# Three banks for scores, the norm factor and the inverse sums through DRAM, and gates ahead of the last branch's products, in a two-layer hybrid encoder

## The chip, the cores and the metric

The kernel runs on one core of a Trainium2 chip. The metric is device time in microseconds (us), lower is better. The time before is 1617.49 us, the median of three runs from 1617.4 to 1617.58. A core has TensorE for matrix products, VectorE (DVE), ScalarE (ACT) and GpSimd (POOL) for elementwise work, and SyncE (SP), which here only issues DMAs. TensorE writes its results into PSUM, which has eight banks of 128x512 float32; other data lie in SBUF.

## The reference

Two layers act on x, which has 512 tokens and 1024 channels, in float32. Per layer:

```python
h = rms_norm(x, attn_norm_g)
c_q, c_kv, k_rope, gq, gk, gv, pool_in, gate_logits = split_columns(h @ w_in, IN_SIZES)
o_mla = mla_branch(...)    # latent attention, 8 heads, keys of 64 + 32 rotary, values of 64
o_gqa = gqa_branch(...)    # grouped attention, 8 heads on 2 key heads of 64, axial rotary
o_pool = pool_branch(...)  # centred means over 2/4/8/16 tokens less the token, a 128x128 map per group
gates = sigmoid(gate_logits).reshape(b, s, 3, d)
merged = (gates[:, :, 0] * (o_mla @ w_branch_mla) + gates[:, :, 1] * (o_gqa @ w_branch_gqa)
          + gates[:, :, 2] * (o_pool @ w_branch_pool))
x = x + merged @ w_out
hf = rms_norm(x, ffn_norm_g)
u = depthwise_conv(hf @ ffn_w_up, ffn_conv_w, ffn_conv_b)      # width 3
x = x + (silu(u[..., :D_FF]) * u[..., D_FF:]) @ ffn_w_down     # D_FF = 2816
```

The attentions are softmax(q k^T / sqrt(d)) v, with a per-head RMS norm on queries and keys. `rms_norm` divides by the root mean square over the channels: one factor per token.

## The kernel before

**Precision.** Each operand of a large product is held as a sum of a high and a low part, and `mm3` issues three matmuls (high x high, high x low, low x high). Weights come from DRAM in pieces of up to 128x512, two to a load as a rule; `w_dma` issues the loads on SP into three rotating buffers (`RAW`), and `w_split` makes the high part on ACT (line 214) and the low part on DVE or POOL (line 221), three pieces ahead of use (`LA`). A load waits until the buffer it takes has been split, and SP runs its DMAs strictly in the order they were written.

**Order.** The program is one long Python function that puts out instructions in an order of its own. A `Clock` keeps planned times for each engine; `chain` puts out the steps of an evacuation one after another as the planned times come, and `ps(tag)` hands out PSUM banks by planned times. The banks have tags: `acc` two, `ST` two, `AV` two, `S` one, `mi` one. The chip takes nothing from the plan but the order on each engine; real waits go by semaphores.

**Stages of a layer.** The latent projection; four pool channel groups; the query, key and value projections; the attentions; the output projection (`w_out`); the up-projection of 44 blocks, which uses `acc`, `ST` and `AV` in turn (six banks); the down-projection. A block of 128 output channels takes 24 matmuls of 128x512 (8 input chunks, three each), on 512 tokens.

**The norm factor.** `norm_finish` sums squares with four small matmuls, takes the mean on DVE and the power -1/2 on POOL (`rt`, one factor per token, with tokens on partitions). Products with channels on partitions need it as a row repeated on all partitions: `rbc`. Before, DVE builds diagonal matrices of the factor's two parts (`dgh`, `dgl`) and `norm_rows` multiplies them with a matrix of ones on TensorE, two matmuls, and copies the result on ACT. There are four such norms. First users: the pool groups' evacuation (`pool_steps`) and `up_evac`.

**The attentions.** `attention` lists, per head, its steps at positions from `PLAN`: `t_q`, `t_k` (operands), `s_max` (scores by query in bank `S`; DVE takes their maxima `nm`, which go as a row through a DMA on ACT's queue), `probs` (four score tiles by key; ACT takes exp, ACT or DVE the high part `ph`, DVE the low part `pl`, and DVE the value sum `vt` of a column that has no room in the value matrix), `av_hi`, `av_lo`, `av_rest` (products with the values in a bank `AV`; the last, with `vt`, closes the head) and `o_out`. In `o_out`, after each second head, DVE transposes the sums of the pair in blocks, takes inverses and transposes them back; POOL multiplies the pair with them (DVE for the last pair) and the pair is split for the branch product.

**Filler.** Between these steps a `Filler` puts units of other work on TensorE: gate blocks (`gate`, 8 units of three matmuls), branch products (`branch`, 4 units), and the latent attention's query, key and value units (`make_q`, `make_n`, `make_v`). Where a step's inputs would not be ready by plan, up to `SLACK` more units are taken. `_order(br)` lists a branch's gates and products; `LAG` is how many gates go ahead of the first product (2: pool branch, 1: grouped, 0: latent, the last). The last figure of each `PLAN` row is the position at which the filler is to be used up. A `make_` unit is woven in at every second unit of the other work.

## Time and profile before

The profiled execution took 1617.62 us, of which the profile's span covers 1615.8. DMA engines moved 161.23 MB, 100 GB/s on average.

| engine | busy us | share of the span | instructions |
|---|---|---|---|
| TensorE matmuls (PE) | 1604.7 | 99% | 7155 |
| TensorE weight loads (PEld) | 1315.5 | 81% | 7155 |
| DVE | 949.8 | 59% | 1548 |
| ACT | 779.0 | 48% | 1407 |
| POOL | 1002.1 | 62% | 889 |

How to read the rows: line numbers are those of the kernel. A row of a group names line, engine, operation, tile written <- tiles read, shapes and count; then the busy time and the mean of one in ns, or min/median/max in ns with the first and last start in us. A row of waits reads "engine, instruction <- whom it waited for: total us, times, longest us". A row of a window reads "from:to length, busy time (instructions), granted clock of TensorE as a share of full speed, busy share of the DMA engines, GB/s"; with more engines, the busy times stand in the order PE, PEld, DVE, ACT, POOL. A row of a timeline reads start, duration, engine, line, operation, tiles, count, and in brackets the idle time before it and what ended it. DMA rows give KB and the median time from issue to landing in us.

### The profile page before, as it was taken

Reading aid. Unit: us, or ns where it says so; the run is one execution under the profiler, and the core shown is the slowest. Engines: PE = TensorE matmul, PEld = TensorE weight load, DVE = VectorE, ACT = ScalarE, POOL = GpSimd, SP = SyncE. Lnnn points to the kernel's source line nnn. Section 1 sums busy time; section 2 is a strip of 40 time slices with the busy share of each in tenths; the row PEclk is TensorE's granted clock in tenths of the full one; section 3 lists DMA queues with packets and bytes.
Section 4 is the critical chain, followed back from the end, with each engine's and each line's share of the span. In section 5 each row is a group of like instructions: output and inputs, shape, how many; then the busy total and the mean of one; then the engine's idle time right before and its main releaser. Section 6 shows DMA issues by size and latency. Waiting matters only on the chain.

```text
span 1615.8 us, 20557 instructions
## 1 busy us (share of the span) xinstructions
PE 1604.7 (99%) x7155; PEld 1315.5 (81%) x7155; DVE 949.8 (59%) x1548; ACT 779.0 (48%) x1407; POOL 1002.1 (62%) x889
## 2 busy tenths in 40 slices
PE   9999999999999999999999999999999999999999
PEld 8888878877888888888888887788778888888888
DVE  6768867865276666611047678777652766666000
ACT  6357766663444444423244576666633444444221
POOL 3764986854666665654477559668547566666542
PEclk9999999999999999999999999999999999999999
DMA  5232234414323223333333322343142222223331
GB/s 194 94 100 71 76 112 127 111 56 143 103 90 93 92 92 102 95 115 101 104 105 94 96 76 75 95 125 118 56 153 92 90 93 92 92 92 104 117 112 46
DMA packets 72104, 161.23 MB, mean 100 GB/s; under 512 B 12224, under 2 KB 33216, under 8 KB 72000
## 3 DMA queue, kind: packets, MB, share of 16 engines
q1 hardware_dynamic: 67104, 159.71, 31.5%
q8 instruction: 56, 0.92, 0.2%
q10 hardware_dynamic: 4896, 0.21, 0.2%
q14 instruction: 48, 0.39, 0.1%
HBM read 147.76 MB, written 12.06 MB: 99 GB/s over the span
## 4 chain that ended last, share of the span: by engine, by line
PE 95%; DVE 2%; POOL 1%; ACT 1%; issue 0%; DMA 0%; ACTq 0%; POOLq 0%; DVEq 0%
PE ps_acc L353 43%; PE ps_ST L353 24%; PE ps_AV L353 23%; PE ps_S L353 4%; PE ps_mi L353 2%; DVE pl L221 0%; DVE vt L225 0%; POOL MQ L221 0%; POOL wl L221 0%; ACT ps_ST L214 0%; ACT ph L214 0%; DVE gt L221 0%; DMA prm<-prm 0%; POOL osum L249 0%; POOL qa L221 0%
## 5 line engine op out<-in xcount | busy, mean ns | idle before, releaser
L221 POOL TENSOR_TENSOR wl<-raw,wh 128x512 fp32r<-128x512 f32 (+2 forms) x502 | 659.1, 1323 | 467.2 <-ACT wh L214 374.5
L214 ACT ACTIVATE wh<-raw 128x512 fp32r<-128x512 f32 (+1 forms) x521 | 309.4, 607 | 131.2 <-PE ps_ST L353 41.0
L225 DVE SCALAR_TENSOR_TENSOR a<-u,prm,a 128x512 f32<-128x512 f32 x176 | 238.8, 1358 | 79.4 <-ACT a L214 75.1
L353 PE MATMUL ps_acc<-HH,wh 128*128 128x512 f32 x592 | 234.2, 396 | 1.3 <-ACT mns L214 1.2
L353 PE MATMUL ps_acc<-HL,wh 128*128 128x512 f32 x592 | 234.5, 396 | 0.0
L353 PE MATMUL ps_acc<-HH,wl 128*128 128x512 f32 x592 | 233.9, 395 | 0.0
L353 PEld LDWEIGHTS ps_acc<-HH,wh 128*128 128x128 f32 x592 | 111.4, 188 | 27.6 <-ACT mns L214 1.4
L353 PEld LDWEIGHTS ps_acc<-HH,wl 128*128 128x128 f32 x592 | 111.2, 188 | 26.6
L353 PEld LDWEIGHTS ps_acc<-HL,wh 128*128 128x128 f32 x592 | 111.3, 188 | 25.7
L353 PE MATMUL ps_AV<-HL,wh 128*128 128x512 f32 x288 | 114.1, 396 | 0.0
L353 PE MATMUL ps_AV<-HH,wl 128*128 128x512 f32 x288 | 114.1, 396 | 0.0
L353 PE MATMUL ps_AV<-HH,wh 128*128 128x512 f32 x288 | 113.4, 394 | 0.0
L214 ACT ACTIVATE ps_ST<-ps_ST 128x512 f32<-128x512 f32 x128 | 74.2, 581 | 81.1 <-PE ps_ST L353 78.1
L221 POOL TENSOR_TENSOR al<-a,ah 128x512 fp32r<-128x512 f32 x44 | 58.1, 1320 | 84.9 <-ACT ah L214 56.5
L229 DVE TENSOR_REDUCE nm<-ps_S 128x1 fp32r<-128x512 f32 x128 | 87.5, 684 | 38.3 <-PE ps_S L353 37.3
L221 DVE TENSOR_TENSOR pl<-ps_ST,ph 128x512 fp32r<-128x512 f32 x128 | 86.6, 681 | 35.1 <-ACT ph L214 34.2
L353 PE MATMUL ps_ST<-HL,wh 128*128 128x512 f32 x240 | 95.2, 397 | 0.0
L353 PE MATMUL ps_ST<-HH,wl 128*128 128x512 f32 x240 | 94.9, 395 | 0.0
L353 PE MATMUL ps_ST<-HH,wh 128*128 128x512 f32 x240 | 94.5, 394 | 0.0
L214 ACT ACTIVATE a<-u,prm 128x512 f32<-128x512 f32 x88 | 71.8, 815 | 33.4 <-DVE u L221 33.4
L214 ACT ACTIVATE ah<-a 128x512 fp32r<-128x512 f32 x44 | 27.8, 632 | 116.0 <-DVE u L249 110.6
L214 ACT ACTIVATE a<-a 128x512 f32<-128x512 f32 x44 | 27.8, 632 | 112.9 <-DVE u L249 112.9
(372 smaller groups left out, 3654.9 us busy)
## 6 DMA issues: line engine op xcount, KB each, us to landing
raw<-w SPq DMA_DIRECT2D x228, 512.0 KB, 3.5
raw<-w SPq DMA_DIRECT2D x13, 384.0 KB, 3.1
XM<-x SPq DMA_DIRECT2D x16, 256.0 KB, 4.0
dtq<-tr SPq DMA_DIRECT2D x16, 192.0 KB, 3.2
dtk<-tr SPq DMA_DIRECT2D x16, 192.0 KB, 4.0
tf<-dtq SPq DMA_DIRECT2D x48, 64.0 KB, 2.8
tf<-dtk SPq DMA_DIRECT2D x48, 64.0 KB, 2.7
raw<-w SPq DMA_DIRECT2D x6, 448.0 KB, 3.4
```

What stands on the lines that cost most here:

```text
L214: return self.eng.activation(out, in_, func, **k)
L221: return self.eng.tensor_tensor(out, *a)
L225: return self.eng.scalar_tensor_tensor(out, *a)
L229: return self.eng.tensor_reduce(out, in_, *a, **k)
L353: PE.matmul(o, lhsT=lhsT, rhs=rhs, start=start, stop=stop)
```

## The change

- *Banks.* `probs` takes its bank from the tag `ST` or `mi`, whichever the plan frees sooner (`soonest`), so three banks serve score tiles. The first step of the value sum (key tile 0) is done by ACT in place of DVE.
- *Norm factor.* `dgh`, `dgl`, `norm_rows` and its matmuls are gone. SP writes `rt` as a row of 512 to DRAM (`row`) and reads it back repeated on 128 partitions into `rbc` (`rows`).
- *Inverse sums.* For the pairs that end with heads 1, 3 and 5, SP writes the two rows of sums to DRAM, reads them as 128x8 (`few`), DVE takes the reciprocal, SP writes it back and reads each row repeated on 64 partitions into `turned`; POOL multiplies with that. The pair of head 7 stays as it was.
- *Filler.* `LAG[0]` is 8 in place of 6: all eight gates of the last branch precede its products. The latent plan's filler ends at 35.5 in place of 33.91. Key and value units are woven in at every fourth unit (`gap`), query units at every second as before.

```diff
@@ -32,7 +32,7 @@
 EXTRA = (("q", 2, (2, 5)), ("n", 2, (6, 7)), ("v", 1, (2, 5)))
 
 SOONER = {1: 3 * KC, 0: 6 * KC}
-LAG = {2: 1, 1: 4, 0: 6}
+LAG = {2: 1, 1: 4, 0: 8}
 PRO = 0.47
 PRE_A = 16
 PRE_B = 8
@@ -41,7 +41,7 @@
 RSQRT_BITS = 1597463007.0
 SLACK = 35
 PLAN = {"gqa": (-4.2, -1.0, -0.2, 0.0, 0.65, 2.411, 4.57, 32.003),
-        "mla": (-6.2, -2.9, -1.0, 0.1, 0.64, 1.678, 1.82, 33.91)}
+        "mla": (-6.2, -2.9, -1.0, 0.1, 0.64, 1.678, 1.82, 35.5)}
 
 D_ROW, D_OUT, D_IN = 3.4, 3.2, 4.0
 REST = 0.4
@@ -228,8 +228,8 @@
         self._two(in_)
         return self.eng.tensor_reduce(out, in_, *a, **k)
 
-    def tensor_scalar(self, out, *a, psum=False):
-        self._count(out, *((0.0043, 0.2) if self.kind == "Pool" else (0.00105 if psum else 0.00055, 0.07)))
+    def tensor_scalar(self, out, *a):
+        self._count(out, *((0.0043, 0.2) if self.kind == "Pool" else (0.00055, 0.07)))
         return self.eng.tensor_scalar(out, *a)
 
     def tensor_copy(self, out, in_, psum=False):
@@ -288,6 +288,13 @@
         uid[0] += 1
         t = pp.tile([P, T], F32, tag=tag, name=f"ps_{tag}_{uid[0]}", bufs=nbank[tag])
         return t
+
+    def soonest(*tags):
+
+        for t in tags:
+            while not banks[t]:
+                ck.pop()
+        return min(tags, key=lambda t: banks[t][0])
 
     def free(tag):
         heapq.heappush(banks[tag], ck.fin + ck.SEM)
@@ -453,30 +460,23 @@
         for b in range(4):
             mm(s2[:, 2 * b:2 * b + 2], sq[:, b * P:b * P + P], f(ones[:, :2]), True, True)
         rt = out["rt"] = small("rt", [P, 8])
-        rh, rl = small("rth", [P, 8], F32R), small("rtl", [P, 8], F32R)
-        dg = out["dg"] = slot("dgh", F32R), slot("dgl", F32R)
+        rbc = out["rbc"] = slot("rbc")
+        d = dp.tile([T], F32, tag=f"rt{gen}", name=f"rt{gen}")
 
         def mean():
             V.tensor_scalar(rt, s2[:, :8], 1.0 / D, EPS, ALU.mult, ALU.add)
             free("S")
 
-        def diag(n):
-            r = f((rh, rl)[n]).rearrange("p (b t) -> p b t", t=2)[:, :, 0:1]
-            V.tensor_tensor(dg[n][:, :T].rearrange("p (b q) -> p b q", b=4), bc(ident[:, None, :], [P, 4, P]),
-                            bc(r, [P, 4, P]), ALU.mult)
-
-        chain(mean, *rsqrt_steps(rt, 8, ("rt", gen)), lambda: V.tensor_copy(rh, rt),
-              lambda: V.tensor_tensor(rl, rt, f(rh), ALU.subtract), lambda: diag(0), lambda: diag(1),
-              lambda: done("dg", gen), after=0.4)
-
-    def norm_rows(gen, out, tag):
-
-        need(("dg", gen))
-        r = ps(tag)
-        for n in range(2):
-            mm(r, ones, out["dg"][n][:, :T], n == 0, n == 1)
-        rbc = out["rbc"] = slot("rbc")
-        chain(lambda: (A.activation(rbc[:, :T], r, AF.Copy), free(tag), done("rbc", gen)))
+        def row():
+            SY.dma_start(d.rearrange("(b p) -> p b", p=P), rt.rearrange("p (b t) -> p b t", t=2)[:, :, 0])
+            ck.fin = ck.now + D_ROW
+
+        def rows():
+            SY.dma_start(rbc[:, :T], d.partition_broadcast(P))
+            ck.fin = ck.now + D_IN
+            done("rbc", gen)
+
+        chain(mean, *rsqrt_steps(rt, 8, ("rt", gen)), row, rows, after=0.4)
 
     def copy(out, in_, psum=True, bias=C_BIAS):
 
@@ -677,8 +677,6 @@
                 if l == 0 and g == 0 and n == 5:
                     norm_finish(G1, sq, nrm)
                     latents()
-            if g == (l == 0):
-                norm_rows(G1, nrm, "acc")
             chain(*pool_steps(g, acc, ptags[g]))
 
 
@@ -884,15 +882,15 @@
                     merged[m] = (mh, ml)
                     chain(product, add, *split(mh[:, :T], ml[:, :T], XM[:, m, :]), fin)
 
-            extra, tick = None, 0
+            extra, tick, gap = None, 0, 2
             for k, m in _order(br):
                 if k in mla_make:
-                    extra, tick = mla_make[k](m), 0
+                    extra, tick, gap = mla_make[k](m), 0, 2 if k == "q" else 4
                     continue
                 work = branch(m) if k == "b" else gate(m)
                 more = True
                 while more:
-                    if extra and tick % 2 == 0:
+                    if extra and tick % gap == 0:
                         if next(extra, END) is END:
                             extra = None
                         yield
@@ -1206,7 +1204,8 @@
                 need(key("m", h), key("q", h))
                 if not gqa:
                     need(key("kl", h))
-                sc = ps("ST")
+                tag = soonest("ST", "mi")
+                sc = ps(tag)
                 kb_ = slice(k * P, k * P + P)
                 if gqa:
                     mm(sc, s["ka"][:, kb_], s["qa"][:, :T], True, False)
@@ -1233,12 +1232,12 @@
 
                     if k == 0:
                         s["t"] = slot("vt", F32R)
-                        V.tensor_scalar(s["t"][:, :T], sc, vals(h, k)[1], None, ALU.mult, psum=True)
+                        A.activation(s["t"][:, :T], sc, AF.Copy, scale=vals(h, k)[1])
                     else:
                         t = s["t"][:, :T]
                         V.scalar_tensor_tensor(t, sc, vals(h, k)[1], f(t),
                                                ALU.mult, ALU.add)
-                    free("ST")
+                    free(tag)
                     if k == 3:
                         done(*key("t", h))
 
@@ -1301,14 +1300,34 @@
                     odst[h // 2] = (oh, ol)
 
                     turned, inv = slot("otr"), small("oinv", [P, 16])
+                if h in (1, 3, 5):
+                    few = small("few", [P, 8])
+                    d1, d2 = (dp.tile([2, T], F32, tag=f"s{n}{kind}{l}{h}", name=f"s{n}{kind}{l}{h}") for n in (1, 2))
+
+                    def line(out, in_):
+                        SY.dma_start(out, in_)
+                        ck.fin = ck.now + D_ROW
+
+                    def both():
+                        for j in range(2):
+                            SY.dma_start(turned[64 * j:64 * j + 64, :T], d2[j].partition_broadcast(64))
+                        ck.fin = ck.now + D_IN
+
+                    steps += [lambda: line(d1, sums[0:65:64, :T]),
+                              lambda: line(few, d1.rearrange("h (a e) -> (h a) e", e=8)),
+                              lambda: V.reciprocal(few, few),
+                              lambda: line(d2.rearrange("h (a e) -> (h a) e", e=8), few), both, add,
+                              lambda: G.tensor_tensor(raw[:, :T], raw[:, :T], turned[:, :T], ALU.mult),
+                              *split(oh[:, :T], ol[:, :T], raw[:, :T], eng=G), lambda: done(okey, l, h // 2)]
+                elif h == 7:
                     steps += [lambda: V.transpose(turned[:, :T], sums[:, :T]),
                               lambda: V.reciprocal(inv, turned[:, :T].rearrange("p (b f) -> p b f", f=32)[:, :, 0])]
                     steps += [add, lambda: (A.activation(inv[32:64], inv[0:32], AF.Copy),
                                             A.activation(inv[96:128], inv[64:96], AF.Copy))]
                     steps += [lambda: V.transpose(sums[:, :T].rearrange("p (b f) -> p b f", f=32),
                                                   bc(inv.unsqueeze(2), [P, 16, 32]))]
-                    steps += [lambda: (V if h == 7 else G).tensor_tensor(raw[:, :T], raw[:, :T], sums[:, :T], ALU.mult),
-                              *split(oh[:, :T], ol[:, :T], raw[:, :T], eng=V if h == 7 else G),
+                    steps += [lambda: V.tensor_tensor(raw[:, :T], raw[:, :T], sums[:, :T], ALU.mult),
+                              *split(oh[:, :T], ol[:, :T], raw[:, :T], eng=V),
                               lambda: done(okey, l, h // 2)]
                 chain(*steps)
 
@@ -1341,14 +1360,15 @@
                 if fn is s_max:
                     return [key("q", h)] + [key("kh", h)] * (not gqa), "S"
                 if fn is probs:
-                    return [key("m", h), key("q", h)] + [key("kl", h)] * (not gqa), "ST"
+                    return [key("m", h), key("q", h)] + [key("kl", h)] * (not gqa), ("ST", "mi")
                 if fn is av_hi:
                     return [key("ph", h, k)], "AV" if k == 0 else None
                 return [key("t", h)] if fn is av_rest else [key("pl", h, k)], None
 
             def waiting(fn, *args):
                 keys, tag = waits(fn, *args)
-                return not ck.has(*keys) or (tag and not (banks[tag] and banks[tag][0] <= ck.now))
+                tags = (tag,) if isinstance(tag, str) else tag or ()
+                return not ck.has(*keys) or bool(tags) and not any(banks[t] and banks[t][0] <= ck.now for t in tags)
 
             f0, first = fill.done, plan[0][0]
             for pos, fn, args in plan:
@@ -1466,8 +1486,6 @@
                 run(feat_major(acc, G2))
                 if n == 1:
                     norm_finish(G2, sq, fin)
-                if n == 2:
-                    norm_rows(G2, fin, "mi")
                 up_evac(c, part, acc, tag)
 
         last = l == L - 1
```

## The prediction

> **What bounds the kernel now.** I read the page first (the busy table, the chain that ended last), then TensorE's own waits, then windows cut around each wait, then the DMA and queue tables.
>
> ```profile
> span 1615.8 us, 20557 instructions
> ...
> PE 1604.7 (99%) x7155; PEld 1315.5 (81%) x7155; DVE 949.8 (59%) x1548; ACT 779.0 (48%) x1407; POOL 1002.1 (62%) x889
> ...
> PE 95%; DVE 2%; POOL 1%; ACT 1%; issue 0%; DMA 0%; ACTq 0%; POOLq 0%; DVEq 0%
> ```
>
> TensorE is the bound: 95% of the chain runs on it. So only two things can shorten the run: fewer matmuls, or fewer stalls between them. The 99% hides part of the stalls, because a matmul counts as busy until its modelled end, so I count starts instead. In each window below the matmuls in brackets include those still draining at its left edge (one; two in 973.68, where they are narrow); the others started in it.
>
> ```profile
> 505.79:517.00 11.21, 11.21 (x49) 1.00 0.29 91
> 240.11:241.17 1.06, 0.40 (x2) 1.00 0.97 397
> 356.23:358.25 2.02, 1.23 (x4) 1.00 0.05 18
> 365.69:367.27 1.58, 1.23 (x4) 1.00 0.00 0
> 973.68:975.47 1.79, 0.61 (x4) 1.00 0.87 119
> 1003.66:1005.11 1.45, 0.97 (x4) 1.00 0.00 0
> 1021.08:1027.26 6.18, 5.25 (x18) 1.00 0.25 86
> 1045.12:1046.16 1.04, 0.40 (x2) 1.00 0.10 24
> 1161.22:1163.25 2.03, 1.24 (x4) 1.00 0.00 0
> 1170.68:1172.27 1.59, 1.24 (x4) 1.00 0.85 268
> ```
>
> The first row is steady work: 48 starts in 11.21 us, 0.2335 us each, at full granted clock (1.00). The stall in another window is its length less 0.2335 per start.
> - 240 and 1045: one start each, 0.83 and 0.81 us lost. This is a latent value unit before its second half.
> - 356 and 1161: three starts, 1.32 and 1.33. The last head of the latent attention.
> - 365 and 1170: three starts, 0.88 and 0.89. The first product of the last branch.
> - 973: two starts, 1.32 (one is half as wide, so a little more). A latent key unit in layer 1.
> - 1003 and 1021: three and 17 starts, 0.75 and 2.21. The end of layer 1's grouped attention.
>
> That is 10.34 us in nine places. Whom TensorE waits for there:
>
> ```profile
> PE ps_AV L353 <- DVE vt L225: 1.7, 3, 0.8
> PE ps_acc L353 <- DVE vm L221: 1.3, 2, 0.7
> PE ps_acc L353 <- ACT mns L214: 1.2, 1, 1.2
> PE ps_ST L353 <- DVE vt L225: 0.5, 1, 0.5
> PE ps_acc L353 <- DVE ol L221: 0.5, 2, 0.2
> ```
>
> All are evacuations of a PSUM bank, or products of one, by DVE or ACT; none is a weight or a DMA.
>
> **The change part by part.**
>
> *Norm factor through DRAM.* Four norms each lose two matmuls of 128x512 that spread the factor over the partitions.
>
> ```profile
> L353 PE MATMUL ps_acc<-dgh,ones x2: 392/392/393, 35.1 to 830.0; 128*128 128x512 f32 x2
> L353 PE MATMUL ps_mi<-dgh,ones x2: 396/398/399, 449.1 to 1254.2; 128*128 128x512 f32 x2
> L221 POOL TENSOR_TENSOR rt<-rt,mhalf x4: 1644/1652/1655, 28.4 to 1248.9; 128x8 f32<-128x8 f32 x4
> L214 ACT ACTIVATE rbc<-ps_acc x2: 577/578/580, 36.4 to 830.9; 128x512 f32<-128x512 f32 x2
> L214 ACT ACTIVATE rbc<-ps_mi x2: 598/599/600, 449.8 to 1254.9; 128x512 f32<-128x512 f32 x2
> ```
>
> They are on the path, in the stream of starts: 8 x 0.2335 = 1.87 us gained. The Trainium skill (TensorE: Matmul & The Clock Gate, "Back-to-back issue gap") gives 512/2.4 + 2.5 = 216 ns for such a step; by it the gain would be 1.73, and the measured step decides. On DVE four casts, four subtractions and eight 128x512 products go, on ACT four copies; neither was waited for. Instead SP issues a write of 512 elements and a broadcast read of 256 KB. Nearest rows:
>
> ```profile
> qb<-nm ACTq DMA_DIRECT2D x16, 2.0 KB, 2.1
> gb<-gb SPq DMA_DIRECT2D x2, 256.0 KB, 4.8
> tf<-dtp SPq DMA_DIRECT2D x24, 64.0 KB, 2.9
> DMA to landing us min/median/max: 1.9/1.9/4.2
> ```
>
> (The last row is that of the tile nm.) In the feed-forward the power ends near 445.5 and the factor came at 450.4. Now the write also waits on SP behind one weight load, up to a block (24 x 0.2335 = 5.6 us), then 1.9 to 4.2 and 2.9 to 4.8: factor at 450.3 to 460.1. The first bank that needs it back is the seventh in turn, six blocks (33.6 us) after 437, so at about 470: cost 0, cover 10 us even at the late end. ACT and DVE are queued behind the late factor and the weight splits stand behind them on ACT; three pieces are split ahead (8.4 us), and the code's own plan already allows 3.4 + 4.0 us for the two hops, so I take 0. At the start of a layer it is tighter, since the latent transposes wait for DVE work queued behind the factor's first use:
>
> ```profile
> 41.42 3.99 DVE L233 TENSOR_SCALAR mx<-mx,ssc 128x256 f32<-128x256 f32 x8 [0.93 <-POOL ssc L221]
> 46.75 1.03 PE L357 MATMUL ps_acc<-C,mx 128*128 128x128 f32 x8
> ```
>
> In layer 0 the power ends at 30, the factor came at 37.0, the transposes at 46.75. In the new order DVE does three products of about 0.68 and these 3.99 us behind the factor, so one later than about 40.5 costs its excess. By the same two landings it comes at 35 to 39, or 41 if the write stands behind a weight load first: 0, at most 1.
>
> *Three banks for scores.* The bank of one tile may be used again when exp, split, remainder and value sum are through:
>
> ```profile
> L214 ACT ACTIVATE ps_ST<-ps_ST 128x512 f32<-128x512 f32 x128 | 74.2, 581 | 81.1 <-PE ps_ST L353 78.1
> L221 DVE TENSOR_TENSOR pl<-ps_ST,ph 128x512 fp32r<-128x512 f32 x128 | 86.6, 681 | 35.1 <-ACT ph L214 34.2
> L233 DVE TENSOR_SCALAR vt<-ps_ST,vg x16: 734/741/743, 121.3 to 1021.0; 128x512 fp32r<-128x512 f32 x16
> L225 DVE SCALAR_TENSOR_TENSOR vt<-ps_ST,vm,vt x48: 664/741/752, 257.4 to 1162.1; 128x512 fp32r<-128x512 f32 x48
> ```
>
> At least 0.58 + 0.6 + 0.68 + 0.74 = 2.6 us. In the old order of TensorE's instructions 9 starts (2.1 us) lie between the closest two users of one bank at the end of layer 1's grouped attention, and 17 (4.0) elsewhere; in the new order at least 24 (5.6). At the end of layer 1's grouped attention the old order runs out of gate matmuls (score, product, score, product with nothing between), since they were spent earlier while it waited for banks; the new order keeps layer 0's pattern there, which lost nothing at the same place. I take the 0.75 + 2.21 as gone.
>
> *First value sum from DVE to ACT.* 32 instructions of 741 ns leave DVE (23.7 us), 32 of about 581 come to ACT (18.6 us). Load in the two attentions of layer 0:
>
> ```profile
> 120.00:225.00 105.00, 104.95 (x472) 87.11 (x471) 88.31 (x155) 77.14 (x146) 76.75 (x95) 1.00 0.24 75
> 250.00:358.00 108.00, 107.21 (x459) 87.36 (x457) 83.82 (x136) 68.22 (x125) 70.37 (x63) 1.00 0.34 98
> ```
>
> DVE was busy 84% of the first, ACT 73%; eight instructions per attention move 5.9 us off DVE and 4.6 us onto ACT: 79% and 78%. Nothing on the path; ACT's share stays below what DVE bore. Cost 0.
>
> *Inverses of the grouped sums through DRAM* (pairs 1, 3 and 5, so 12 times). Gone from DVE: two block transposes and a wide reciprocal.
>
> ```profile
> L245 DVE STREAM_TRANSPOSE otr<-osum x16: 669/699/714, 154.4 to 1164.1; 128x512 f32<-128x512 f32 x16
> L241 DVE RECIPROCAL oinv<-otr x16: 230/238/254, 156.1 to 1164.8; 128x16 f32<-128x16 f32 x16
> ```
>
> 12 x (2 x 0.70 + 0.24) = 19.7 us of DVE, for a smaller reciprocal; POOL's product stays. New are five DMAs on SP, in a row: row out, columns back, inverse out, two broadcasts back. On the path none: the results are wanted by the next branch's products two heads later (28 us), and four hops of 1.9 to 4.2 make 17 at most. The danger is what stands behind a late hop. DVE's reciprocal waits for the second, POOL's product for the fourth, the weight loads behind them on SP, and SP's own longest wait is:
>
> ```profile
> SPq L307 <- POOL wl L221: 1158.5, 238, 11.0
> ```
>
> A weight load on SP waits 4.9 us on average (1158.5/238) for POOL, and in the new order a load stands between two hops in nearly all 12 chains. The code places the reciprocal 3.4 us after the hop that feeds it, a hop lands in 1.9, so a hold of 1.5 us is free. Most of the 4.9 us passes before a hop is due, since SP reaches the load early. I charge 1.4 us to the whole: six waits of about 0.25 us behind DVE, as TensorE's bank for score maxima is reused 5 starts later and little slack lies there. Ends: 0 (all covered) and 12 x 1.7 = 20 us (half of the full 4.9 + 1.9 - 3.4 = 3.4 reaches TensorE).
>
> *All gates ahead of the last branch's products* (lag 8, and the plan's end at 35.5). Old order after the last head: 24 gate matmuls, then the first product, whose fourth operand came after 33 starts and 0.88 us of stall, 8.6 us. New order: 69 gate matmuls first, so 78 starts, 18.2 us. The 0.88 and 0.89 go. Because more filler is left over, 22 starts (5.1 us) instead of 10 lie between the last score tile and the head's closing matmul; the old ten and their stall made 2.3 + 1.3 = 3.6, so the 1.32 and 1.33 go as well. What is late next: the eight products in a row, 2.8 us each for two banks; seven stood in a row before, with no stall in the waits. Cost 0.
>
> *Latent units spread wider.* Between the two halves of a value unit lay 7 starts (1.6 us) and 0.83 of stall: 2.5 needed; now 14 (3.3). In 973 a gate took the key unit's own bank right behind it, and stood until ACT had read it (mns). In the new order every gate behind a key unit waits for DVE alone, so for the other bank, freed by the product before; the closest of these pairs is 5 starts (1.17 us) apart, and the old order has one like it in layer 0, near 177, without a stall. The 0.83, 0.81 and 1.32 go.
>
> **Sum.** 1.87 + 10.34 = 12.2 us gained, 1.4 lost to new waits: 10.8. The profiled execution took 1617.62 us (its span and 1.8 around it), 0.01% over the median of 1617.49. 1617.6 - 10.8 = **1606.8 us**.
>
> **The rivals.**
> 1. *The stalls in the middle of the attentions come back elsewhere.* Only what is fixed by counting stays: 1.87 + 2.65 (last heads) + 1.77 (first products) = 6.3, **1611.3**. For it: every order put out by the same plan leaves places of its own where real and planned times part, and layer 1's 2.96 us has no twin in layer 0 though the plan is nearly the same. Against: nearly every distance in the new order is longer.
> 2. *SP holds the hops and DVE stands still* (the other side). If a hop is held 3.4 us beyond plan in each chain and half reaches TensorE, 12 x 1.7 = 20 us: 1605.4 + 20 = **1625**. It decides at 15.4/12 = 1.3 us per chain (12.2 gained, and 0.2% = 3.2). For it: the mean hold of 4.9. Against: the key and query transposes already go out and back over this queue between the same loads, and no DMA is among TensorE's waits.
> 3. *Small pieces land late.* If each of the three small hops takes the longest row, 4.2, instead of 1.9, it is 0.8 over plan each, 2.4 per chain; half of it 12 times is 14: **1620**. Beside it stands the Trainium skill (DMA: Bandwidth & Descriptors, "Specifications"): pieces under 512 bytes are read, modified and written; these have 32 bytes. The row speaks against it so far: pieces of 16 bytes landed in 1.9 at the median.
> 4. *The hops cost just what is gained*, about 1 us per chain: **1617**.
>
> **How the numbers follow.** Forecast 0.62 (its own range 1604 to 1610), rival 1 0.17, rivals 2 and 3 together 0.12, rival 4 0.07, and 0.02 for less than 1604. The range 1604 to 1614 holds the first two. A change under 0.2% (3.2 us) could hardly be told from none: faster 0.62 + 0.17 + 0.02 = 0.81, same 0.07, slower 0.12.
>
> **What would show it.** The matmuls of dgh gone and no wait on rbc; the same windows after the last heads and at the first products free of stalls; no wait of scores' banks on vt; engine waits named few or otr small. It is wrong if DVE or POOL shows waits of microseconds on DMA few or otr, if TensorE waits for nm or the maxima's bank, or if weights (wl) come late.

## The result and the profile after

The change made the kernel slower. Its time is 1642.93 us (median of six, 1638.25 to 1648.14) against 1617.31 us (1616.73 to 1617.58) for the kernel before, run beside it: a ratio of 1.016, with a 95% interval of 1.0141 to 1.0178, so 25.6 us are lost. The prediction was 1606.8 us, with a range up to 1614. The profiled execution of the changed kernel took 1644.36 us.

The page of the changed kernel (the busy times, the chain by engine), and behind it a row of its table of DMAs:

```profile
PE 1613.7 (98%) x7147; PEld 1318.2 (80%) x7147; DVE 902.4 (55%) x1479; ACT 785.8 (48%) x1405; POOL 1012.4 (62%) x892
...
PE 81%; POOL 5%; issue 5%; DMA 4%; DVE 2%; ACT 1%; SPq 1%; ACTq 0%; POOLq 0%; DVEq 0%
...
rt<-rt SPq DMA_DIRECT2D x4, 2.0 KB, 10.6
```

The eight matmuls are gone (7147 in place of 7155) and DVE has 47 us less to do, as intended. But of the chain only 81% lies on TensorE, where it was 95%; POOL, DMAs and issue took the rest. The last row names the first suspect: the small row of the factor lands 10.6 us after its issue. The waits of the changed kernel (engine, instruction <- whom it waited for: total us, times, longest):

```profile
PE ps_S L360 <- DVE nm L229: 6.1, 4, 3.3
PE ps_acc L360 <- DVE vm L221: 5.3, 2, 3.0
PE ps_acc L364 <- DVE mx L233: 3.8, 1, 3.8
...
DVE u L221 <- DMA rbc<-rt: 34.6, 2, 17.8
ACT vt L214 <- DVE pl L221: 18.6, 22, 2.4
DVE pp L221 <- DMA rbc<-rt: 11.7, 1, 11.7
DVE few L241 <- DMA few<-s1mla: 10.7, 4, 3.7
DVE few L241 <- DMA few<-s1gqa: 6.0, 2, 4.3
```

TensorE itself still waits for no DMA. Its waits are for DVE, and DVE waits for DMAs: 46.3 us for the factor (`rbc`) and 16.7 us for the sums (`few`). The row of ACT's `vt` is a wait that did not exist before. Three places of the changed kernel's timeline show how it goes. First the factor in layer 0, then in its feed-forward, then a chain of sums at the end of layer 1's grouped attention:

```profile
31.19 0.43 SPq L471 DMA_DIRECT2D rt<-rt  x1
42.62 0.33 SPq L475 DMA_DIRECT2D rbc<-rt  x1
47.47 1.32 DVE L221 TENSOR_TENSOR pp<-ps_AV,rbc 128x512 f32<-128x512 f32 x2 [11.71 <-DMA rbc<-rt]
...
475.72 0.69 DVE L221 TENSOR_TENSOR u<-ps_acc,rbc 128x512 f32<-128x512 f32 x1 [17.82 <-DMA rbc<-rt]
479.28 1.50 POOL L221 TENSOR_TENSOR wl<-raw,wh 128x512 fp32r<-128x512 f32 x1 [14.04 <-ACT wh L214]
...
1002.41 0.50 SPq L1308 DMA_DIRECT2D s1gqa<-osum  x1
1009.96 0.32 SPq L314 DMA_DIRECT2D raw<-w  x1
1010.38 0.38 SPq L1308 DMA_DIRECT2D few<-s1gqa  x1
1013.75 0.20 DVE L241 RECIPROCAL few<-few 128x8 f32<-128x8 f32 x1 [4.32 <-DMA few<-s1gqa]
1014.56 0.63 PE L360 MATMUL ps_S<-ka,qa 128*128 128x512 f32 x1 [3.29 <-DVE nm L229]
```

In layer 0 the factor is there at 47.5, where it came at 37.0 before. In the feed-forward DVE stands 17.8 us for it, the weight splits stand behind ACT's work on the same blocks, and POOL idles 14 us. In the third part SP waits at 1002.9 to 1010 with a weight load whose buffer is not free, and the hop written behind that load goes out at 1010.38, eight microseconds after the first hop. Standing right behind that load, it also takes 3.4 us until DVE goes on. DVE's reciprocal waits for it, the score maxima `nm` wait behind the reciprocal, and TensorE for their bank.

Windows of the changed kernel (length, TensorE busy, granted clock) round two of these places, and then over layer 0's last latent head, whose closing product starts at 367.6, and over the first product of the last branch, at 384, where the kernel before had a stall each:

```profile
46.00:58.00 12.00, 8.30 (x27) 0.72 0.20 78
1010.50:1020.00 9.50, 6.21 (x20) 0.82 0.33 84
356.00:370.00 14.00, 14.00 (x62) 1.00 0.32 95
370.00:392.00 22.00, 22.00 (x96) 1.00 0.37 107
```

The last two rows are without a stall. The first two show something new: after the long waits the granted clock is down, and matmul starts come 0.427 us apart in place of 0.2335.

### The profile page after: what moved, and what is told of

Its sections match the earlier page's. It is cut to its first block, busy times and chain, and to the rows that moved or that the text cites. A ratio compares the mean times of both kernels' runs of the same rounds, so it can differ in the third digit from the quotient of the medians.

```text
span 1642.6 us, 20548 instructions
## 1 busy us (share of the span) xinstructions
PE 1613.7 (98%) x7147; PEld 1318.2 (80%) x7147; DVE 902.4 (55%) x1479; ACT 785.8 (48%) x1405; POOL 1012.4 (62%) x892
## 4 chain that ended last, share of the span: by engine, by line
PE 81%; POOL 5%; issue 5%; DMA 4%; DVE 2%; ACT 1%; SPq 1%; ACTq 0%; POOLq 0%; DVEq 0%
PE ps_acc L360 37%; PE ps_AV L360 20%; PE ps_ST L360 19%; PE ps_S L360 3%; POOL wl L221 3%; PE ps_mi L360 2%; DMA rt<-rt 1%; DMA raw<-w 1%; DVE XM L221 1%; DMA few<-s1mla 1%; POOL al L221 0%; SPq L1085 0%; POOL win L221 0%; DMA tf<-dtq 0%; DVE nm L229 0%
## 5 line engine op out<-in xcount | busy, mean ns | idle before, releaser
L221 POOL TENSOR_TENSOR wl<-raw,wh 128x512 fp32r<-128x512 f32 (+3 forms) x505 | 669.6, 1337 | 486.3 <-ACT wh L214 383.8
L225 DVE SCALAR_TENSOR_TENSOR a<-u,prm,a 128x512 f32<-128x512 f32 x176 | 234.7, 1338 | 86.3 <-ACT a L214 82.4
L214 ACT ACTIVATE ps_ST<-ps_ST 128x512 f32<-128x512 f32 x86 | 50.1, 582 | 53.4 <-PE ps_ST L360 50.4
L214 ACT ACTIVATE HH<-XM,prm 128x512 fp32r<-128x512 f32 x32 | 23.2, 724 | 106.3 <-DVE XM L221 55.0
```

Of the source, the lines that this page charges most:

```text
L214: return self.eng.activation(out, in_, func, **k)
L221: return self.eng.tensor_tensor(out, *a)
L225: return self.eng.scalar_tensor_tensor(out, *a)
```

## The experiments

All times are medians, beside the kernel before on the same chip (1616.94 to 1617.4).

| run | what it is | us | ratio to before, 95% interval |
|---|---|---|---|
| e1 | changed, factor on TensorE again | 1625.28 | 1.0041 to 1.0071 |
| e2 | changed, inverses on DVE again | 1626.95 | 1.0043 to 1.0073 |
| e3 | changed, both undone | 1613.61 | 0.9968 to 0.9987 |
| e4 | before, factor through DRAM | 1628.3 | 1.0052 to 1.0082 |
| e5 | e4, row in 128-byte pieces | 1614.71 | 0.9975 to 0.9994 |
| e6 | e1, hops on ACT's queue | 1615.79 | 0.9985 to 1.0004 |
| e7 | before, filler's part | 1618.3 | 0.9999 to 1.0018 |
| e8 | before, third bank and value sum on ACT | 1615.93 | 0.9984 to 1.0003 |
| e9 | e3 with the factor as in e5 | 1612.36 | 0.9960 to 0.9983 |
| e10 | e9, value sum on DVE | 1606.87 | 0.9925 to 0.9950 |
| e11 | e4, matmuls in the wait | 1629.97 | 1.0066 to 1.0094 |
| e12 | changed, with the mends of e5 and e6 | 1616.86 | 0.9990 to 1.0008 |
| e13 | changed, value sum on DVE | 1625.21 | 1.0035 to 1.0065 |
| e14 | before, third bank | 1609.77 | 0.9938 to 0.9971 |
| e15 | e12, value sum on DVE | 1615.78 | 0.9983 to 1.0002 |
| e16 | e9, value sum ahead of `pl` | 1610.14 | 0.9941 to 0.9971 |
| e17 | e10 without the filler's part | 1608.17 | 0.9928 to 0.9961 |

### Undoing one way through DRAM (e1, e2, e3), or doing it alone (e4)

e1 puts `norm_rows` and the diagonal matrices back into the changed kernel, e2 the transposes in `o_out`, e3 both; e4 puts the row and its broadcast into the kernel before.

```diff
# e1
-        def row():
-            SY.dma_start(d.rearrange("(b p) -> p b", p=P), rt.rearrange("p (b t) -> p b t", t=2)[:, :, 0])
...
+        rh, rl = small("rth", [P, 8], F32R), small("rtl", [P, 8], F32R)
...
+                norm_rows(G1, nrm, "acc")
# e2
-                              lambda: line(few, d1.rearrange("h (a e) -> (h a) e", e=8)),
...
+                    steps += [lambda: V.transpose(turned[:, :T], sums[:, :T]),
```

> The changed kernel with the norm factor made on TensorE again (diagonal matrices and two matmuls per norm); banks, inverse sums and filler stay as changed. In the changed kernel the excess of matmul starts over their steady step is about 7 to 8 us at 45 to 57, 3.5 at 864 to 880, 2.5 at 480 to 495 and 1.7 at 1302 to 1310, some 16 us, all at places behind a norm factor. Theory 1 (the write of the factor in four-byte pieces lands after about 10 us and holds up DVE, ACT and POOL behind it): these places go, eight matmuls (1.9 us) come back, so about 1629 us. Rival A (those places come from the inverse sums' DMAs or from the new order as such): they stay, about 1643 to 1645 us.

> The changed kernel with the inverses of the pairs of heads 1, 3 and 5 made on DVE again by block transposes; the norm factor through DRAM, the banks and the filler stay as changed. In the changed kernel the attentions hold some 22 us of excess starts (4 at 256, 5 at 1011 to 1018, 4.5 at 1073 to 1080, the rest in pieces of 1 to 2). Theory 2 (the DMAs of the inverse sums stand behind weight loads on SP and hold up DVE and ACT): most of that goes, about 1622 us. Rival B (the new order, the three banks and the first value sum on ACT make these stalls): they stay, 1638 us or more.

> The changed kernel with both ways through DRAM undone, so only the three banks, the first value sum on ACT, the gates ahead and the wider spread are left of the change. Theories 1 and 2 together: about 1607 us (the kernel before less the stalls of 10.3 us that these parts were to remove). Rival B: 1620 us or more, with the stalls at 256, 1011 and 1073 still there.

> The kernel before with the norm factor through DRAM as the only change. Theory 1: 16 us of stalls behind the four norms, less 1.9 of matmuls, so about 1631 us. Rival A (this part costs nothing by itself): 1615.5 us.

Measured: 1625.28, 1626.95, 1613.61 and 1628.3. So the factor through DRAM costs 11.1 us alone (e4 less before), 13.3 beside the other parts (e2 less e3) and 17.7 in the full change (after less e1). The inverses cost 11.7 (e1 less e3) and 16.0 (after less e2). Both theories hold, though the sizes were off: e1 fell more than expected (1629) and e2 less (1622). What neither explains is e3: 1613.6 in place of 1607, so the rest of the change loses some 6 us of its own.

### Why the factor is late (e5)

```diff
-            SY.dma_start(d.rearrange("(b p) -> p b", p=P), rt.rearrange("p (b t) -> p b t", t=2)[:, :, 0])
+            V.transpose(rtt, rt32)
+            for q in range(4):
+                SY.dma_start(d.rearrange("(b q j) -> q b j", q=4, j=32)[q], rtt[32 * q:32 * q + 8:2, :])
```

> The kernel before with the norm factor through DRAM alone, but DVE first turns the 128x4 factors in blocks of 32x32, so that the row is written in 16 pieces of 128 bytes by four DMAs on SP, in place of 512 pieces of four bytes by one. With the four-byte pieces alone the time was 1628.3 us, and the write stood 10.9 us between issue (31.28) and the issue of the broadcast that waits for it (42.16). Theory 1 (the four-byte pieces make the landing late): the write lands in 1.5 to 4 us, the factor comes at about 40 in layer 0, and the time is 1616 to 1618 us (eight matmuls saved, small waits left). Rival (a hop through DRAM is late behind the weight loads whatever its pieces): 10 us again, and 1626 us or more.

Measured: 1614.71 us, a little better than expected. The timeline of e4 (512 pieces of four bytes), and behind it that of e5 (16 pieces of 128):

```profile
31.28 0.43 SPq L464 DMA_DIRECT2D rt<-rt  x1
42.16 0.34 SPq L468 DMA_DIRECT2D rbc<-rt  x1
46.89 1.32 DVE L221 TENSOR_TENSOR pp<-ps_AV,rbc 128x512 f32<-128x512 f32 x2 [11.03 <-DMA rbc<-rt]
```

```profile
31.28 2.51 SPq L468 DMA_DIRECT2D rt<-rtt  x4
35.76 0.33 SPq L472 DMA_DIRECT2D rbc<-rt  x1
39.10 1.32 DVE L221 TENSOR_TENSOR pp<-ps_AV,rbc 128x512 f32<-128x512 f32 x2 [3.27 <-DMA rbc<-rt]
```

Same place, same issue time, same 2 KB, nothing between the two DMAs on SP: the write took 10.9 us in four-byte pieces and 4.5 (2.5 of them for issuing four DMAs) in 128-byte pieces. The pieces are the cause and not the queue; whether it is their number or their size was not separated, since both change together. With 128-byte pieces the route through DRAM is worth 2.4 us (1.0 to 4.0 by the interval), which agrees with the 1.87 of its eight matmuls. DVE still stands for `rbc` in e5, 9.3 us at the longest, in the feed-forward, and TensorE waits for nothing there: up to that length the wait is covered.

### Why the inverses are late (e6)

```diff
                     def line(out, in_):
-                        SY.dma_start(out, in_)
+                        nc.scalar.dma_start(out, in_)
...
-                            SY.dma_start(turned[64 * j:64 * j + 64, :T], d2[j].partition_broadcast(64))
+                            nc.scalar.dma_start(turned[64 * j:64 * j + 64, :T], d2[j].partition_broadcast(64))
```

> The changed kernel with the norm factor on TensorE again (1625.28 us) and, as the one further change, the five DMAs of each inverse-sum chain issued on ACT's queue in place of SP's. Theory 2a (on SP the hops stand behind weight loads that wait for a buffer, and other transfers behind the hops): the waits of DVE on few (15.7 us in 6) and of ACT on tf shrink to a few us and the time falls to 1611 to 1615 us, where it is without these hops (1613.61). Rival 2b (the chain of hops is too long whatever queue it is on): 1622 us or more. Rival 2c (ACT, which then waits in order for the hops, becomes the late engine): new waits of TensorE on ACT, over 1618 us.

Measured: 1615.79 us, 9.5 less than e1 and just over the expected band. DVE's waits for `few` in e1 (its profiled execution took 1630.01 us, 4.7 over its median), and then what is left in e6:

```profile
DVE few L241 <- DMA few<-s1mla: 10.0, 4, 3.3
DVE few L241 <- DMA few<-s1gqa: 5.7, 2, 4.3
```

```profile
ACT tf L214 <- DMA tf<-dtq: 10.8, 4, 5.1
...
PE ps_acc L360 <- DVE vm L221: 3.4, 2, 2.1
```

In e6 there is no row of DVE waiting for `few` at all. So SP's queue held the hops. The hops themselves are quick there (1.4 to 1.9 us each, from issue to landing). On SP, in the changed kernel, they took 1.4 to 3.7 us, with a median of 3.3: of the six that DVE waited for, the four issued within 2 us of a weight load took 2.8 to 3.7, and the two issued 3.8 and 7.6 us behind one took 1.6 and 2.0. The other half of the theory fell: ACT's wait for `tf` stayed (11.1 us in e1), so the hold on SP was not what delayed those transfers. The trace of e15, below, points to the order that the plan gives around the hops.

### The other parts alone (e7, e8, e14)

```diff
# e7
-LAG = {2: 1, 1: 4, 0: 6}
+LAG = {2: 1, 1: 4, 0: 8}
...
+                    extra, tick, gap = mla_make[k](m), 0, 2 if k == "q" else 4
# e8 and e14
-                sc = ps("ST")
+                tag = soonest("ST", "mi")
+                sc = ps(tag)
# e8 only
-                        V.tensor_scalar(s["t"][:, :T], sc, vals(h, k)[1], None, ALU.mult, psum=True)
+                        A.activation(s["t"][:, :T], sc, AF.Copy, scale=vals(h, k)[1])
```

> The kernel before with only the filler's part of the change: lag 8, the latent plan's end at 35.5, key and value units at every fourth unit. Theory 3 (each stall of the prediction's list goes with the part that it was put down to): 0.83 + 0.81 + 1.32 + 1.32 + 1.33 + 0.88 + 0.89 = 7.4 us less, about 1610 us. Rival (a new order has stalls of its own in places where the old one had none, as at 153, 318 and 956 in the run with both ways through DRAM undone): 1612 to 1616 us.

> The kernel before with only the three banks for scores and the first value sum on ACT. Theory 3: the stalls at the end of layer 1's grouped attention (0.75 + 2.21) go and nothing comes, about 1614.3 us. Rival (they go and others come, at the branch products and last heads that the run with both ways undone shows): 1616 to 1619 us.

> The kernel before with only the third bank for scores; value sum on DVE, filler, norm factor and sums as before. Theory as in the prediction (the third bank takes 0.75 + 2.21 us of stalls at the end of layer 1's grouped attention): about 1614.3 us. If it also removes the stalls at the last heads, which the filler alone left in place: about 1611.5 us. If the gain of 10 us of the best run needs the filler's part: 1616 us or more.

Measured: 1618.3, 1615.93 and 1609.77. The third bank alone gives 7.5 us, more than any of its expectations said, and the filler alone gives nothing, less than either said. Windows over the last heads, of e7 (layer 0; 1163.3 to 1165.4 in layer 1 is alike) and then of e14 (both layers):

```profile
356.55:358.57 2.02, 1.25 (x5) 1.00 0.02 6
```

```profile
345.00:360.00 15.00, 15.00 (x66) 1.00 0.20 71
1140.00:1165.00 25.00, 25.00 (x109) 1.00 0.19 64
```

With all the filler left over, the stall at the last head is still there in e7; with the third bank it is gone in e14, where the filler's order is the old one. TensorE's waits of e7, and of e14, show what changed:

```profile
PE ps_AV L353 <- DVE vt L225: 1.8, 4, 0.8
PE ps_acc L353 <- ACT mns L214: 1.2, 1, 1.2
```

```profile
PE ps_acc L360 <- DVE vm L221: 1.3, 2, 0.7
PE ps_S L360 <- DVE nm L229: 1.1, 1, 1.1
```

The two waits for `vt` at the last heads (0.75 us each) are in e7 and not in e14. The timelines show why: between the last score tile of that head and its closing product, which needs `vt`, lie 10 other matmul starts before and in e7, and 25 in e14. So the third bank lets the score tiles run ahead, and `vt` is ready when the head closes; the filler left over does not do it. In e14 the stalls at the first products are gone too, with the old six gates ahead of them. What is left there of the nine stalls of the prediction are the two at the latent value units (0.83 and 0.82 us), and one of 1.5 us at 308, behind score maxima, is new. Between e8 and e14 stands one instruction per head, the first value sum: on ACT it costs 6.2 us.

### The first value sum (e9, e10, e13, e16)

e9 is e3 with the factor as in e5. e10 and e13 take the sum back to DVE, e10 in e9 and e13 in the changed kernel. e16 leaves it on ACT but puts it ahead of DVE's remainder `pl`:

```diff
-                chain(ex, hi, lo, ([("vg", l, k) if gqa else ("vm", l, k, h // 4)], rest))
+                summed = ([("vg", l, k) if gqa else ("vm", l, k, h // 4)], rest)
+                chain(ex, hi, *((summed, lo) if k == 0 else (lo, summed)))
```

> The changed kernel with the inverse sums on DVE as before, and the norm factor through DRAM written in 16 pieces of 128 bytes after a block transpose. If the parts add, as the single runs have it (both ways undone 1613.61; the 128-byte rows took 2.4 off the kernel before): about 1611.2 us, the fastest so far. If the rows' gain is taken by other stalls of the new order: 1613 us or more.

> As the run with banks, filler and 128-byte rows, but the first step of the value sum stays on DVE. Theory (ACT, with the value sum added, comes late with mqs, and the three stalls of 0.98 us at 153, 956 and 972 come from that): they go, and about 2 to 3 us less than that run, some 1608 to 1609 us. Rival (DVE, busier by 5.9 us per attention, comes late with the score maxima and the banks): equal or slower, 1611 us or more.

> The changed kernel with only the first step of the value sum back on DVE; both ways through DRAM stay as changed. Moving that step saved 5.5 us where neither way through DRAM disturbed (1612.36 to 1606.87). Theory (this step on ACT costs about the same in the changed kernel): about 1637.5 us. Rival (in the changed kernel DVE is the late engine, behind the hops and the factor, and its extra load eats the gain): 1641 us or more.

> As the run with banks, filler and 128-byte rows and the first value sum on ACT (1612.36 us), with one order changed: ACT makes that sum right behind the high part, ahead of DVE's remainder pl of the same score tile, in place of behind it. There ACT stood 19.7 us in 23 of the 32 sums until pl had been read out of the bank, and exp, high parts and bank evacuations stood behind it. Theory (this wait in ACT's queue is what the move to ACT costs): the 5.5 us come back, 1607 to 1609 us. Rival (it is ACT's 0.69 us of work itself): 1612 us. Rival (now pl waits for ACT, and DVE with it): over 1612 us.

Measured: 1612.36, 1606.87, 1625.21 and 1610.14. So the sum on ACT costs 5.5 us where nothing else disturbs, twice what was expected, and 17.7 us in the changed kernel, three times what was expected there. Waits of e9 (`mqs` is the copy of a latent query unit out of its bank), then of e16, and all of TensorE's waits of e10:

```profile
ACT vt L214 <- DVE pl L221: 20.7, 23, 2.3
...
PE ps_acc L360 <- ACT mqs L214: 1.6, 2, 0.8
```

```profile
DVE pl L221 <- ACT vt L214: 5.8, 8, 1.7
```

```profile
PE ps_mi L1536 <- DVE ones L249: 1.1, 1, 1.1
PE ps_S L360 <- DVE nm L229: 1.0, 1, 1.0
PE ps_acc L360 <- DVE wh L237: 0.7, 1, 0.7
PE ps_acc L360 <- DVE vm L221: 0.6, 1, 0.6
```

In 23 of the 32 sums ACT stands until DVE has read `pl` out of the same bank, 0.9 us each (the 19.7 us of e16's expectation are those of e3), though neither reads what the other writes; exp, high parts and bank evacuations stand behind it. The Trainium skill (PSUM — Partial Sum Buffer, "PSUM bank collisions raise a hardware error") says that two engines may not be in the same partitions of one bank at the same time, two readers included, and that accesses to a bank are to be kept apart by semaphores; the waits agree with it in both orders. Turned round in e16, the wait is DVE's and much smaller, and 2.2 of the 5.5 us come back. So the wait is part of the cost and not all; what makes up the rest, DVE's new wait or ACT's own 0.69 us per sum, was not separated. Why the sum costs 17.7 us in the changed kernel is not shown as a whole. One part can be read in e13: with the sum to do, DVE comes to the hops later and stands only 4.8 us for `few` in place of 16.7, and TensorE waits 0.8 us for `nm` in place of 6.1, though the hops are still on SP. e10 is the fastest kernel of this study, 10.1 us under before.

### The parts mended (e12, e15, e17)

e12 is the changed kernel with the mends of e5 and e6; e15 moves its value sum to DVE as well; e17 takes the filler's part out of e10.

```diff
# e17
-LAG = {2: 1, 1: 4, 0: 8}
+LAG = {2: 1, 1: 4, 0: 6}
...
-                    extra, tick, gap = mla_make[k](m), 0, 2 if k == "q" else 4
+                    extra, tick = mla_make[k](m), 0
```

> The whole change kept, with two mends: the norm factor's row is written in 16 pieces of 128 bytes, and the hops of the inverse sums go over ACT's queue. If what made the change slow is the four-byte pieces and the hops' place on SP, and nothing else: 1615.79 (hops on ACT's queue, factor on TensorE) less 2.4, about 1613.4 us. If the two ways through DRAM hinder each other in some other way (together they cost 4.3 us more than each by itself): 1617 us or more.

> The fastest run so far (1606.87 us: three banks, value sum on DVE, filler, 128-byte rows) with the inverse sums through DRAM over ACT's queue in place of DVE's transposes; that is the whole change but for the value sum's engine, the queue and the rows' pieces. DVE loses 19.7 us of work by it. Theory (the inverses through DRAM are worth nothing even where nothing holds them): 1606.5 to 1609 us. Rival (they relieve a DVE that carries the value sum): under 1606 us. Rival (the stalls of value units at 214, 250 and 1050, as in the mended run of 1616.86 us, belong to the hops): 1611 us or more.

> The fastest run (1606.87 us) without the filler's part: three banks, value sum on DVE, 128-byte rows. If the filler's part is worth nothing once the banks are there: 1609.77 (third bank alone) less 2.4 for the rows, 1607.4 us, the same within the measurement. If the filler's part is worth the 7.4 us that its places in the kernel before suggest: about 1614 us.

Measured: 1616.86 (from 1615.0 to 1619.38), 1615.78 and 1608.17. The two mends take 26.1 us off the changed kernel and bring it back to where it was before, 3.5 us above what was expected if nothing else was wrong. Inverses through DRAM, on ACT's queue, cost 2.2 us with the factor on TensorE (e6 less e3), 4.5 with the factor in 128-byte rows and the sum on ACT (e12 less e9), and 8.9 where everything else is at its best (e15 less e10), with DVE waiting for `few` only 0.2 us. ACT's and TensorE's waits of e15, and what stands ahead of them in its timeline:

```profile
ACT tf L214 <- DMA tf<-dtq: 12.7, 3, 5.8
...
PE ps_acc L360 <- DVE vm L221: 5.1, 2, 2.8
...
228.89 1.09 POOL L249 MEMSET osum<- 1x512 f32 x2
230.01 0.69 DVE L221 TENSOR_TENSOR oraw<-oraw,osum 128x512 f32<-128x512 f32 x1 [4.44 <-POOL osum L249]
232.49 0.64 ACT L214 ACTIVATE oh<-oraw 128x512 fp32r<-128x512 f32 x1 [4.99 <-DVE oraw L221]
```

The two long waits are at 246 and 1048, in the latent value units: ACT stands 5.3 and 5.8 us for a transposed operand (`tf`), and the bank's copy `vm` behind it. That is the place that e6 left over, and TensorE's two waits make 5.1 of the 8.9 us. The timelines of e15 and e10 show where the lateness begins. In the changed code POOL's addition for the pair of heads 4 and 5 (`add`) is written behind the hops; it runs at 227.7 in e15 and at 212.6 in e10. The clearing of `osum` for the last pair is written behind it on POOL and ends at 230.0 in place of 225.6, DVE's addition for the last pair waits for that, ACT, in order, waits for DVE (4.99 us; 3.14 in e10), and the DMAs of the transposed operand on SP come 4 to 5 us later (written out at 235.19 and not 230.61). The same two waits of 4.4 to 4.5 and 5.0 us stand in e1, e6, e12 and the changed kernel. So the traces point to the place of this addition in the order; no run moved it back to test that. The filler's part is worth 1.3 us once the third bank is there (e17 less e10), with intervals that overlap.

### The clock after a wait (e11)

```diff
             cT = ps(ctags[j])
+            for _ in range(14 if l == 0 and j == 0 else 0):
+                PE.matmul(cT, lhsT=ones, rhs=ones[:, None, :].to_broadcast([P, 4, P]), start=True, stop=True)
```

> The kernel before with the norm factor through DRAM in four-byte pieces (1628.3 us), and 14 more matmuls of ones in layer 0, put ahead of the latent transposes into the bank that these will overwrite, so that TensorE is at work during most of the 3.3 us in which it waits for mx; nothing else is moved. Without them the 16 matmul starts after that wait came 0.427 us apart, twice the steady step, and the transposes 0.21 to 0.46 us apart, which cost some 3 us on top of the wait. Theory (an idle stretch of TensorE of some 3 us brings its clock down for a while after): the starts behind the wait come at the steady step, and 2.5 to 3 us less: 1625.5 us. Rival (the slow steps have to do with the transposes or their operands, not with the idle time): still there, 1628 us or more.

Windows of e4 and then of e11:

```profile
45.00:50.00 5.00, 1.66 (x7) 1.00 0.54 199
50.00:55.00 5.00, 4.83 (x18) 0.66 0.01 3
```

```profile
45.00:50.00 5.00, 4.07 (x18) 1.00 0.75 247
50.00:55.00 5.00, 4.16 (x22) 1.00 0.01 2
```

The clock stayed up, so the idle stretch was what brought it down. But the time did not fall: 1629.97 us, 1.7 more than e4. In the profiled execution the row landed 1.5 us later than in e4 (12.4 after its issue), so the transposes started 1.3 us later (50.46), and a new wait of 0.9 us for a weight ended at 62.6. What the kept clock is worth by itself can therefore not be read from this run. That the slow clock ran inside time that was lost anyway is how I read it, and it is not shown.

## Why the prediction was wrong

One path through the runs, from the kernel before to the changed one, splits the loss: third bank -7.5 (e14), first value sum to ACT +6.2 (e8), filler -2.3 (e3), factor through DRAM +13.3 (e2), inverses through DRAM +16.0 (after). These steps end at the measured loss by construction; what each is worth depends on what is already there, as the sum's 5.5 to 17.7 us show.

- **The bound, and stalls as starts less 0.2335 us: right.** The nine stalls were real (that none was for a weight holds but for 0.3 us for `wh` at the kernel's start). In e10 seven of them are gone, the two at the latent value units are smaller (0.3 and 0.7 us), one of 1.4 us at 308 is new, and the time, 1606.87, is the 1606.8 that the prediction gave to the whole change. It got there with two parts of the change undone and one mended, so this is no credit to the sum.
- **Norm factor, "I take 0": the step that failed first.** The gain of 1.87 was right. The bound of the landing, 1.9 to 4.2 us, was taken from the rows of `nm`, which move as many bytes in 128 pieces of 16 bytes inside SBUF; this write to DRAM has 512 pieces of four, and it took 11.4 (10.9 in e4). DRAM as the target is not the reason: the hop that writes the inverses there in 128 pieces of 32 bytes lands in 1.4 in e6. Bytes were compared, and pieces were not counted. The limit was stated correctly, "one later than about 40.5 costs its excess": the factor came at 47.5, seven microseconds over that, and TensorE waited 3.8 us for `mx` and then ran at the lowered clock. In the feed-forward the error was another one. The power ended at 459.6 (the mean at 457.9 and POOL's 1.65), so the factor at 475.7 is 16.1 us behind it, only 1.5 beyond the late end of the range given (445.5 to 460.1). That is luck: SP came to the write after 1.7 us where up to 5.6 was allowed, and the write took 9.1 where 4.2 was. The cover of 10 us was read from the banks, and what ran out first were the weight splits behind ACT: 14 us of POOL idle against 8.4 us split ahead.
- **Inverse sums, 1.4 us charged: 11.7 to 16.** The danger was named, and the upper end of 20 and rival 2 (1625) held the truth. The step that failed is "most of the 4.9 us passes before a hop is due": here the load was written between two hops of one chain, so it was reached late, and the whole hold lay on the second hop (8 us at 1002). Rival 2 was the right mechanism with too small a chance. Rival 3, late small pieces, saw a true sign and gave it the wrong reason: the hops did land late (a median of 3.3 us against the 1.9 assumed), but the same 32-byte pieces land in 1.4 to 1.9 us on ACT's queue in e6, so the weight loads just ahead of them on SP fit as the reason, and the size does not. Late pieces were true of the factor's write, where they were not looked for. And "On the path none" left out that the pair's addition on POOL moved behind the hops, with the last pair's work behind it (e15). The rule of the Trainium skill cited there puts all pieces under 512 bytes in one class (DMA: Bandwidth & Descriptors, "Specifications"); e4 and e5 differ by 6 us within that class.
- **First value sum, "Cost 0": +5.5 alone, +17.7 in the change.** Only busy shares were compared. The step adds a wait to ACT's queue, and what stands behind it was not named; the 0.58 us per sum was also 0.69 here. Why it costs three times as much in the full change is shown only in part (e13).
- **Three banks: gain too small.** 7.5 us (e14) against 2.96. The last heads (2.65) were put down to the filler left over, which was to put 22 starts between the last score tile and the closing product; with the filler alone (e7) there are 10, as before, and with the bank alone (e14) 25. The stalls at the first products and at the key unit go with the bank too. What the counting from bank to bank left out is that score tiles that run ahead make `vt` ready sooner.
- **Gates ahead and wider units: right about the first products (1.77), wrong about the last heads, the key unit and the value units.** The first products' stalls are gone in e7, but the bank alone removes them as well. In e7 the wait of 1.2 us for `mns`, the key unit's copy, is still there; in e14 it is gone. The value units lose 0.7 and 1.3 us in e7, where 0.83 and 0.81 were to go. Alone the filler's part gains nothing, since stalls of its own appear (rival 1); after the third bank it gains 1.3 to 2.3, with intervals that overlap.
- **The signs of being wrong that it named** all came: DVE stood 16.7 us for `few`, TensorE 6.1 for `nm` and, in six waits, 3.9 for late weights (`wl`).

## What to carry to other kernels

Look at the pieces of a small DMA, their number and size, and not at its bytes alone: a block transpose that makes rows of 128 bytes turned a loss of 11 us into a gain of 2.4. A hop on an in-order queue costs what the transfers written ahead of it wait for, so look where loads fall between the hops of a chain, and test it by moving the hops to another queue. When an instruction moves to another engine, look first at what it must wait for there, a bank that another engine reads as well, and only then at the busy shares.

## What was not expected of the hardware

- A DMA that writes 512 pieces of four bytes from 128 partitions let the broadcast behind it go 8.8 to 12.4 us after its issue, in each of the four norms of the changed kernel, e2, e4, e11 and e13; 128 pieces of 16 bytes land in 1.9 (the rows of `nm`, inside SBUF), and 128 pieces of 32 bytes, written to DRAM, in 1.4 (`s2gqa` in e6).
- After some gaps of two to four microseconds between matmul starts TensorE's granted clock falls (0.66 to 0.82 in the windows shown) and matmul starts come 0.427 us apart, for some two to six microseconds. The length of the wait does not decide it alone: in e1 a gap of 2.05 us between starts at 1027 was followed by slow steps, in e15 one of 3.2 us at 1048 was not, as the windows of these two, in this order, show:

```profile
1026.50:1034.50 8.00, 6.23 (x24) 0.79 0.19 50
```

```profile
1047.50:1056.50 9.00, 6.17 (x27) 1.00 0.74 220
```

The Trainium skill (TensorE: Matmul & The Clock Gate, "Part 1: The HAM clock gate") gives an idle window of some 3.4 us after which the clock is halved. The granted clock of 0.50 from 1030.3 to 1033.1 in e1 agrees with it; that gaps of two microseconds can do it, and longer ones need not, is what these runs add.
